# Layer 1 of a two-layer decoder: gates and half of the values by seven block products, all values through DRAM

## The chip, the core and the metric

The kernel runs on one core of a Trainium2 chip. The metric is the device time of one execution in microseconds. A difference of about 0.2% is what a measurement of this kernel can tell from no change.

The names used below are those of the profile: PE is TensorE (matmuls), PEld its weight loads, DVE is VectorE, ACT is ScalarE, POOL is GpSimd, and SP is SyncE, which here only issues DMAs.

## What is computed

Two layers over 512 rows of width 1024. Layer 1 is a differential attention of 16 heads, layer 2 a spatial gating MLP. The change is in layer 1:

```python
h = rms_norm(x, attn_norm)                       # 512 x 1024
proj = h @ w_in                                  # 1024 x 8192: q, k, v, gate, 2048 columns each
q, k, v, gate = ...                              # 16 heads; q and k hold two halves of 64, v is 128 wide
s  = softmax(q1 @ k1.T * scale + bias) - lam * softmax(q2 @ k2.T * scale + bias)   # causal
o  = rms_norm(s @ v, subln) * (1 - lam_init)
x  = x + (o * silu(gate)) @ w_out
```

All data are float32. Each product with a weight is made of three: both operands are cut into a high part (`hi`) and the rest (`lo`), and hi·hi + lo·hi + hi·lo is summed in PSUM.

## The kernel before

**Weights.** A weight comes from DRAM in chunks of 1 MB, in two halves (tile `raw`, three halves held). ACT rounds each of four pieces to `hi` (L134) and DVE makes `lo = raw - hi` (L135). There are three `hi`/`lo` pairs. `Chunk.tick` spreads the four pieces of the next chunk over the matmuls of the present one.

**Stages of layer 1.** `norm_rows` makes `hT` (hi and lo of the normed rows, turned). Then: `project_values(0)`, the values of heads 0 to 3 (96 matmuls of 512 columns, L423); `project_qk(0)`, q and k of heads 0 and 1 (96 matmuls, L253 to L255, tile `psqk`); the gate loop, 16 blocks of 24 matmuls into `psg`, each ended by a SiLU into `yT` (L501 to L506); then eight pairs of heads.

**A pair of heads.** `attention_steps` (L606) lays five groups of score blocks over ten slots: in slot t `scores` of group t (tile `pss`, L562), in slot t+2 `flip` (transposes of the finished weights, tile `pa`, L589), in slot t+3 `values` (tile `po`, L600); after `values` of the last group of a head `normalise` runs, and `close` (transposes of `on`, tile `pto`, L540) stands in slot 6 for the first head and in slot 9 for the second. I number the events: scores 0 to 4, flip 0 to 4, values 0 to 4, close 1 and close 2. Between PE's `scores` and `flip` of a group lies the softmax: DVE adds the bias and takes the maximum (L572), ACT takes the exponential (L575), DVE takes the reciprocal, scales and subtracts (L579 to L583). Between `values` and `close` lie four squares on ACT (L530), eleven small DVE operations that make a reciprocal root (L185 to L197), and one product into `on` (L534).

**Filler.** `interleave` (L620) puts projections for later heads between the slots, in units of three matmuls. Pairs 1 to 6 get 48 units each: 32 of `project_qk` for the next pair and 16 of `project_values` (`units`, L643), pairs 7 and 8 get 40, from `last_units`. The q and k results are written by ACT (`qkh`, L446) and DVE (`qkl`, L447). A scheduler then fixes one order of instructions for each engine before the run; each engine works its list off in that order. In the list, close 1 of pairs 1 to 7 follows values 3 at once.

**Block products.** Layer 2 already makes its input projection with `Quads` and seven products for each 1024 columns in the place of eight (the Strassen-Winograd form): a 512 by 512 quarter of the weight is loaded, sums and differences of quarters are made by DVE and by accumulating POOL DMAs (`quarter<-quarter`, 1 MB each), each form is cut into `hi` and `lo` (L344, L345), and the rows' sums `s1` to `s4` are made once. `product_n` has 24 matmuls of 512 columns, `product_t` 48 of 256 columns (L881).

Of the kernel before, what the change touches and what calls it, by code (L numbers as in the profile page):

```python
# [50 lines left out]
def build(ctx, tc, x, rel_bias, attn_norm, w_in, lq1, lk1, lq2, lk2, subln, w_out,  # L51
# [36 lines left out]
    v_at, qk_at = {0: add_values(0)}, {0: add_pair(0)}  # L88
    gate_at = len(chunks)
    for c in range(NH // 2):  # L90
        chunks.append(in_src(w_in, 3 * BR + c * 2 * P))
    for p in range(1, NH // 2):
        qk_at[p] = add_pair(p)
        if p % 2 and p < NH // 2 - 1:
            v_at[p // 2 + 1] = add_values(p // 2 + 1)
# [10 lines left out]
    limit = [sgu_at]  # L106
# [123 lines left out]
    def norm_rows(r, b):  # L230

        rs = row_scale(r, b, r > 0)
        xs = yT[:, 4 + 2 * (b % 2):6 + 2 * (b % 2), :].rearrange("p k n -> p (k n)")
        for m in range(2):
            ms = slice(m * S, (m + 1) * S)
            xs_last[0] = nc.vector.scalar_tensor_tensor(xs[:, ms], xr[:, b, ms], rs, gb[:, ms], ALU.mult, ALU.mult)
        sl = slice(b * P, (b + 1) * P)
        for q in range(KD // 4):
            pt = bank("ptx")
            for j in range(4):  # L240
                k = 4 * q + j
                nc.tensor.transpose(pt[:, j * P:(j + 1) * P], xs[:, k * P:(k + 1) * P], ident)
            pq = pt.rearrange("p (j n) -> p j n", n=P)
            hi_last[0] = nc.scalar.copy(hT[0][:, 4 * q:4 * q + 4, sl], pq)  # L244
            hT_last[0] = nc.vector.tensor_tensor(hT[1][:, 4 * q:4 * q + 4, sl], pq, hT[0][:, 4 * q:4 * q + 4, sl].bitcast(F32),
                                    ALU.subtract)

# [10 lines left out]

    def proj_n(ps, w, b, lo_last=False):

        bs = slice(b * P, (b + 1) * P)
        terms = ((0, w.hi), (0, w.lo), (1, w.hi))
        if lo_last:
            order = [(k, t) for t in (0, 2) for k in range(KD)] + [(k, 1) for k in range(KD)]
        else:
            order = [(k, t) for k in range(KD) for t in range(3)]
        n = len(order)
        for i, (k, t) in enumerate(order):
            a, m = terms[t]
            nc.tensor.matmul(ps, lhsT=hT[a][:, k, bs], rhs=m[:, k, :], start=(i == 0), stop=(i == n - 1))  # L270
            if i % 6 == 5:
                w.tick()
                yield
# [29 lines left out]


# [97 lines left out]
    def project_values(g, blocks, norm=None):  # L402

        i0 = v_at[g]
        if norm is not None:
            prepare(norm, 0)
            with tc.issue_after(xs_last[0].ins):
                for piece in range(PIECES):
                    split(i0, piece)
        if blocks[0] == 0:  # L410
            V[g] = att.tile([P, NB, S], F32, name="v"), [Chunk(i0, 8), None]
        v, w = V[g]
        for two in (blocks[i:i + 2] for i in range(0, len(blocks), 2)):
# [16 lines left out]
            for b in two:  # L430
                nc.scalar.copy(v[:, b, :], ps[b])
# [20 lines left out]
    run(project_qk(0))  # L452
# [7 lines left out]
    lt = yT[:, 12, 0:4 * HALF].rearrange("p (i h) -> p i h", i=4)  # L460
    for i, t in enumerate((lq1, lk1, lq2, lk2)):
        nc.scalar.dma_start(lt[:, i, :], t.broadcast_to([P, HALF]))
    lj = yT[:, 12, 4 * HALF:5 * HALF]
# [24 lines left out]
    oh = yT[0:NBUCK + 1, 0:2, :].rearrange("p k n -> p (k n)")[:, 0:TLEN]  # L488
    nc.scalar.dma_start(oh, onehot)
    tb = dram.tile([NH, TLEN], F32, name="tb")  # L490
    for c in range(2):
# [3 lines left out]
        tbs = yT[0:NH, 10 + c, 0:TLEN // 2]  # L495
# [5 lines left out]
    for c in range(NH // 2):  # L501
# [10 lines left out]
    class Head:  # L512
        def __init__(self, h):
            self.h = h
            qk, self.v = QK[h // 2], V[h // 4][0]
# [27 lines left out]
    class Group:  # L543
# [49 lines left out]
        def values(self):  # L593
            for hd, i, cs in self.parts:
# [68 lines left out]

    def sgu_quarter(n):
        def of(name):
            r, c = divmod("abcd".index(name), 2)
            return wide_src(sgu_w_in, r, columns[n] + c * S)[0]
        return of
# [10 lines left out]
    quads = Quads(qp, [sgu_quarter(n) for n in range(len(columns))])  # L679
# [5 lines left out]
    H = S // 2  # L685
    first = yT[:, 12:16, :].rearrange("p k n -> p (k n)").rearrange("p (k n) -> p k n", n=H)

    gb = yT[:, 6:8, :].rearrange("p k n -> p (k n)")
    last_mm = []
# [25 lines left out]

    def of_h(q, half):
        return [h[:, 4 * q:4 * q + 4, half * H:(half + 1) * H] for h in hT]

    def part(hi, lo, raw):
        nc.scalar.copy(hi, raw)  # L720
        nc.vector.tensor_tensor(lo, raw, hi.bitcast(F32), ALU.subtract)
# [52 lines left out]
    def product_n(ps, a, w, start):  # L774

        more = {} if start else {"skip_group_check": True}
        for i in range(2):
            rs = slice(i * P, (i + 1) * P)
            for k in range(4):
                nc.tensor.matmul(ps[i], lhsT=a[0][:, k, rs], rhs=w[0][:, k, :], start=(start and k == 0), stop=False, **more)  # L780
                nc.tensor.matmul(ps[i], lhsT=a[0][:, k, rs], rhs=w[1][:, k, :], start=False, stop=False, **more)
                last_mm[:] = [nc.tensor.matmul(ps[i], lhsT=a[1][:, k, rs], rhs=w[0][:, k, :], start=False,
                                               stop=(k == 3), **more)]
                yield

# [89 lines left out]
    def product_t(ps, a, w, start):  # L875

        for f in range(4):
            for k in range(4):
                for t, (x, y) in enumerate(((0, 0), (0, 1), (1, 0))):
                    clear = start and f % 2 == 0 and k == 0 and t == 0  # L880
                    nc.tensor.matmul(ps[f // 2][:, f % 2 * H:(f % 2 + 1) * H], lhsT=w[x][:, k, f * P:(f + 1) * P],  # L881
                                     rhs=a[y][:, k, :], start=clear, stop=(k == 3 and t == 2),
                                     skip_group_check=not (start and f % 2 == 0))
                yield

# [129 lines left out]
```

## Time and profile before

| what | value |
|---|---|
| median of 3 runs | 925.95 us (925.34 to 926.55) |
| the profiled execution | 928.58 us, its span 926.8 us |
| PE busy | 904.7 us, 98% of the span |
| DVE busy | 598.2 us, 65% |
| ACT busy | 446.1 us, 48% |
| granted PE clock, mean | 0.997 |

The profiled execution took 2.6 us more than the median of the runs; 1.8 us of it lie outside its span. PE's busy time is made of pipelined records whose ends are modelled, so a busy PE can hold short waits. Start-to-start distances tell more: within the gate loop a matmul starts every 0.227 us. All times of events below are microseconds from the start of the span.

### The profile page before, as it was taken

The page shows a single profiled execution, that of the slowest core. Times are in us where ns is not written, and L with a number is a line of the kernel's source. Part 1 is how long each engine was busy: PE and PEld are TensorE (multiplying, and loading weights), DVE is VectorE, ACT ScalarE, POOL GpSimd, SP SyncE. Part 2 cuts the span into 40 slices and gives each one's busy share as a digit, 9 for nine tenths or more (in the row PEclk, how much of TensorE's full clock was granted, in tenths as well). Part 3 has the DMA queues.
Part 4 walks back from the last instruction along what each step waited for, and adds up shares of the span by engine and source line. Part 5 has one row for each costly group of instructions (what it writes and reads, how often), then busy time and mean ns, then how long its engine had stood idle before and what let it go on. Part 6 is the DMA issues. An engine that isn't in the chain of part 4 may idle for free.

```text
span 926.8 us, 13474 instructions
## 1 busy us (share of the span) xinstructions
PE 904.7 (98%) x5129; PEld 768.6 (83%) x5129; DVE 598.2 (65%) x1359; ACT 446.1 (48%) x995; POOL 24.9 (3%) x38
## 2 busy tenths in 40 slices
PE   7999999999999999999999999999999999999996
PEld 4878887878787878787778887687999999998885
DVE  6532225666766676667777838885887777776634
ACT  6432225545454545454655616664554435454432
POOL 0000000000000000000000002000000000000000
PEclk9999999999999999999999999999999999999998
DMA  7433223213221332132212704647465564534202
GB/s 249 131 104 119 91 91 92 69 49 112 91 69 50 111 92 69 52 108 92 69 46 92 272 1 114 171 105 222 94 200 99 181 138 136 115 114 147 88 17 91
DMA packets 57904, 100.75 MB, mean 109 GB/s; under 512 B 3741, under 2 KB 28366, under 8 KB 56304
## 3 DMA queue, kind: packets, MB, share of 16 engines
q1 hardware_dynamic: 53216, 79.70, 26.5%
q0 software_dynamic: 3568, 18.88, 9.2%
q10 hardware_dynamic: 1056, 1.32, 0.5%
q8 instruction: 40, 0.66, 0.3%
q14 instruction: 24, 0.20, 0.1%
HBM read 85.17 MB, written 2.14 MB: 94 GB/s over the span
## 4 chain that ended last, share of the span: by engine, by line
PE 81%; DVE 10%; DMA 4%; ACT 3%; issue 1%; SPq 0%; ACTq 0%; POOLq 0%; DVEq 0%
PE psv L423 10%; PE px L881 10%; PE py L881 7%; PE psqk L253 6%; PE psqk L255 6%; PE psqk L254 6%; PE acc L289 5%; PE acc L288 5%; PE acc L290 5%; PE pss L562 3%; PE psg L253 3%; PE psg L254 3%; PE psg L255 3%; PE po L600 3%; DMA quarter<-quarter 3%; DVE lo L345 2%
## 5 line engine op out<-in xcount | busy, mean ns | idle before, releaser
L135 DVE TENSOR_TENSOR lo<-raw,hi 128x512 fp32r<-128x512 f32 x192 | 124.4, 687 | 104.4 <-ACT hi L134 104.2
L134 ACT CAST hi<-raw 128x512 fp32r<-128x512 f32 x192 | 109.4, 619 | 104.2 <-PE psqk L254 44.2
L345 DVE TENSOR_TENSOR lo<-quarter,hi 128x1024 fp32r<-128x1024 f32 x84 | 102.2, 1242 | 44.4 <-ACT hi L344 39.8
L344 ACT CAST hi<-quarter 128x1024 fp32r<-128x1024 f32 x84 | 85.9, 1047 | 93.0 <-DMA quarter<-quarter 36.6
L253 PE MATMUL psqk<-hT,hi 128*128 128x512 f32 x256 | 104.3, 408 | 0.0
L575 ACT ACTIVATE e<-e,nm 128x384 f32<-128x384 f32 (+3 forms) x128 | 70.6, 553 | 67.6 <-DVE nm L572 67.6
L255 PE MATMUL psqk<-hT,lo 128*128 128x512 f32 x256 | 100.2, 392 | 0.0
L254 PE MATMUL psqk<-hT,hi 128*128 128x512 f32 x256 | 99.9, 390 | 0.0
L423 PE MATMUL psv<-hi,hT 128*128 128x512 f32 x256 | 87.3, 408 | 1.9 <-ACT hT L244 1.9
L288 PE MATMUL acc<-hi,hT 128*128 128x512 f32 x224 | 88.1, 393 | 0.0
L290 PE MATMUL acc<-hi,hT 128*128 128x512 f32 x224 | 87.4, 390 | 0.0
L289 PE MATMUL acc<-lo,hT 128*128 128x512 f32 x224 | 87.3, 390 | 0.0
L881 PE MATMUL py<-hT,hi 128*128 128x256 f32 x384 | 69.9, 284 | 0.0
L572 DVE CUSTOM_DVE_ANT_0 e<-pss,bias 128x384 f32<-128x384 f32 (+3 forms) x128 | 55.7, 488 | 17.6 <-PE pss L562 17.4
L423 PEld LDWEIGHTS psv<-hi,hT 128*128 128x128 f32 x256 | 49.2, 192 | 15.4 <-ACT hT L244 2.5
L881 PEld LDWEIGHTS py<-hT,hi 128*128 128x128 f32 x384 | 59.8, 192 | 0.0
L253 PEld LDWEIGHTS psqk<-hT,hi 128*128 128x128 f32 x256 | 48.1, 188 | 13.0 <-issue 2.6
L255 PEld LDWEIGHTS psqk<-hT,lo 128*128 128x128 f32 x256 | 48.0, 188 | 10.5
L254 PEld LDWEIGHTS psqk<-hT,hi 128*128 128x128 f32 x256 | 48.2, 188 | 8.9
L881 PE MATMUL py<-hT,lo 128*128 128x256 f32 x192 | 54.3, 283 | 0.0
L283 DVE TENSOR_TENSOR hT<-yT,hT 128x512 fp32r<-128x512 f32 x56 | 37.5, 689 | 25.8 <-PE acc L289 17.3
L282 ACT CAST hT<-yT 128x512 fp32r<-128x512 f32 x56 | 33.1, 621 | 38.3 <-PE acc L289 28.2
(198 smaller groups left out, 1921.1 us busy)
## 6 DMA issues: line engine op xcount, KB each, us to landing
raw<-in_attn_w_in SPq DMA_DIRECT2D x62, 512.0 KB, 3.9
quarter<-in_sgu_w_in SPq DMA_DIRECT2D x48, 512.0 KB, 4.9
quarter<-quarter POOLq DMA_DIRECT2D x12, 1024.0 KB, 7.3
raw<-in_attn_w_out SPq DMA_DIRECT2D x16, 512.0 KB, 3.5
raw<-in_sgu_w_out SPq DMA_DIRECT2D x16, 512.0 KB, 3.6
bias<-tb POOLq DMA_DIRECT2D x16, 256.0 KB, 3.6
xr<-in_x SPq DMA_DIRECT2D x4, 512.0 KB, 5.0
out_y<-xr SPq DMA_DIRECT2D x8, 256.0 KB, 2.1
```

What stands on the lines that cost most here:

```text
L134: nc.scalar.copy(hi[:, sl], raw)
L135: nc.vector.tensor_tensor(lo[:, sl], raw, hi[:, sl].bitcast(F32), ALU.subtract)
L253: nc.tensor.matmul(ps, lhsT=w.hi[:, k, cs], rhs=hT[0][:, k, :], start=(k == 0), stop=False)
L254: nc.tensor.matmul(ps, lhsT=w.hi[:, k, cs], rhs=hT[1][:, k, :], start=False, stop=False)
L255: nc.tensor.matmul(ps, lhsT=w.lo[:, k, cs], rhs=hT[0][:, k, :], start=False, stop=(k == KD - 1))
L288: nc.tensor.matmul(acc[b], lhsT=yh[:, j, bs], rhs=w.hi[:, j, :], start=(k == 0), stop=False)
L289: nc.tensor.matmul(acc[b], lhsT=yh[:, j, bs], rhs=w.lo[:, j, :], start=False, stop=False)
L290: nc.tensor.matmul(acc[b], lhsT=yl[:, j, bs], rhs=w.hi[:, j, :], start=False, stop=(k == KB - 1))
L344: nc.scalar.copy(hi[:, sl], raw[:, sl])
L345: nc.vector.tensor_tensor(lo[:, sl], raw[:, sl], hi[:, sl].bitcast(F32), ALU.subtract)
L423: nc.tensor.matmul(ps[b], lhsT=hT[a][:, k, bs], rhs=m[:, j, :], start=(k == 0 and a == 0 and m is w[half].hi), stop=(k == KD - 1 and a == 1))
L881: nc.tensor.matmul(ps[f // 2][:, f % 2 * H:(f % 2 + 1) * H], lhsT=w[x][:, k, f * P:(f + 1) * P], rhs=a[y][:, k, :], start=clear, stop=(k = ...
```

## The change

Columns of the gates (2048) and of the values of heads 8 to 15 (1024) are now made in three passes of `Quads`, seven products each: pass 0 (values) with `product_n`, passes 1 and 2 (gates) with `product_t`. The row sums for it are made by the new `row_sums` beside the values of heads 4 to 7. All values are made ahead of the attention. They are put into `yT`, stored to DRAM (`vd`, four DMAs of 1 MB from POOL's queue) and fetched again for four heads at a time (`fetch_values`, 1 MB, POOL's queue). The order of stages is now: values 0 to 3, values 4 to 7, three passes of block products, `project_qk(0)`, eight pairs. The filler of pairs 1 to 6 is `project_qk` alone, 32 units.

```diff
-    v_at, qk_at = {0: add_values(0)}, {0: add_pair(0)}
...
+    v_at = {g: add_values(g) for g in range(2)}
+    qk_first = len(chunks)
+    qk_at = {p: add_pair(p) for p in range(NH // 2)}
...
+            if b < 2:
+                nc.scalar.copy(first[:, 4 * q:4 * q + 4, hs], pq)
...
+    def row_sums(b):
...
+        nc.scalar.copy(t, pq[1])
+        nc.vector.tensor_tensor(t, pq[0], t, ALU.add)
+        nc.vector.tensor_tensor(u, f[:, 0:4], t, ALU.subtract)
...
+    def save_values(g):
+        nc.gpsimd.dma_start(vd[g], yT[:, 4 * g:4 * g + 4, :].rearrange("p k n -> p (k n)"))
...
-                nc.scalar.copy(v[:, b, :], ps[b])
+                nc.scalar.copy(yT[:, 4 * g:4 * g + 4, b * P:(b + 1) * P], of_bank(ps[b]))
+        save_values(g)
...
-    run(project_qk(0))
...
+    quads = Quads(qp, [columns_of(w_in, n0) for n0 in (2 * BR + D, 3 * BR, 3 * BR + D)])
+    beside(project_values(1, range(NB)), (u for g in (row_sums(2), row_sums(3), quads.work(0), quads.work(1)) for u in g))
...
-    for c in range(NH // 2):
-        w = Chunk(gate_at + c, 16)
-        for j in range(2):
-            ps = bank("psg")
-            run(proj_t(ps, w, j))
-            nc.scalar.activation(yT[:, 2 * c + j, :], ps, AF.Silu)
+    for n in range(3):
+        gates, m = n > 0, n - 1
...
+        for i in range(7):
+            work = quads.work(7 * n + i + 2)
...
+            product = product_t if gates else product_n
+            beside(product(py if i in (1, 3, 6) else px, sides[i], quads.forms[n, i], i in (0, 1, 3)), work)
...
+        if not gates:
+            for g in (2, 3):
+                save_values(g)
...
+    def fetch_values(g):
+        V[g] = att.tile([P, 4, NB, P], F32, name="v")
+        nc.gpsimd.dma_start(V[g].rearrange("p j b n -> p (j b n)"), vd[g])
+
+    fetch_values(0)
+    run(project_qk(0))
...
+        if p % 2 and p < NH // 2 - 1:
+            fetch_values(p // 2 + 1)
         if p < NH // 2 - 1:
-            interleave(steps, units(p), 48)
+            interleave(steps, project_qk(p), 32)
```

The scheduler lays all lists anew. Three places show what the pairs get. On DVE, in pair 3, from the last step of group 4's softmax (`e`) to the chain that ends in `on` of the first head (`rv`, `ry`, `ru` are its small tiles, `lo` a piece of a weight chunk). Before:

```order
L583 SCALAR_TENSOR_TENSOR e_2291<-e_2292,r_2304,e_2291 128x128
L447 SCALAR_TENSOR_TENSOR qkl<-psqk,qkh 128x512
L197 TENSOR_SCALAR rv_2344<-ssq 128x4
L185 TENSOR_SCALAR ry_2346<-rv_2344 128x4
L190 TENSOR_TENSOR ru_2347<-ry_2346,rv_2344 128x4
L191 TENSOR_TENSOR ru_2347<-ru_2347,ry_2346 128x4
```

and after the change (its lines differ, its names do not):

```order
L715 SCALAR_TENSOR_TENSOR e_2868<-e_2869,r_2881,e_2868 128x128
L505 SCALAR_TENSOR_TENSOR qkl<-psqk,qkh 128x512
L130 TENSOR_TENSOR lo<-raw,hi 128x512
L192 TENSOR_SCALAR rv_2916<-ssq 128x4
L180 TENSOR_SCALAR ry_2918<-rv_2916 128x4
L130 TENSOR_TENSOR lo<-raw,hi 128x512
L185 TENSOR_TENSOR ru_2919<-ry_2918,rv_2916 128x4
L130 TENSOR_TENSOR lo<-raw,hi 128x512
L186 TENSOR_TENSOR ru_2919<-ru_2919,ry_2918 128x4
L130 TENSOR_TENSOR lo<-raw,hi 128x512
L187 SCALAR_TENSOR_TENSOR ry_2918<-ru_2919,ry_2918 128x4
```

Four `lo` pieces have moved from the place ahead of group 4's softmax (L135 at 262.80 in the trace) to behind it, three of them into the chain itself; pairs 2 to 6 read alike.

On PE, in the same pair, around close 1. Before:

```order
L255 MATMUL psqk<-hT_103,lo 128x512
L589 MATMUL pa<-ident,e_2291 128x128 x4
L600 MATMUL po<-v,at 128x128 x4
L540 MATMUL pto<-flip,on 128x128 x4
L253 MATMUL psqk<-hT_103,hi 128x512
```

and after:

```order
L254 MATMUL psqk<-hT_103,hi 128x512
L255 MATMUL psqk<-hT_104,hi 128x512
L256 MATMUL psqk<-hT_103,lo 128x512
L672 MATMUL pto<-flip,on 128x128 x4
L732 MATMUL po<-v,at 128x128 x4
L254 MATMUL psqk<-hT_103,hi 128x512
```

Close 1 now stands nine filler matmuls behind flip 4 and values 3, and just ahead of values 4. From scores 0 of the pair to the next pair's, the runs of filler matmuls have now 9, 9, 9, 9, 12, 9, 9, 20 and 10 (before: 12, 15, 15, 15, 15, 12, 15, 30 and 15). They stand ahead of scores 1, flip 0 with scores 2, flip 1 with scores 3, flip 2 with scores 4, flip 3, flip 4, close 1 (before: values 4), close 2 and the next scores 0.

On POOL, whose list is its DMA queue, from the constants to layer 2. Before:

```order
masks.py:199 ISA
masks.py:199 AFFINE_SELECT ident<-ident 128x128
L523 DMA bias<-tb 128x512 x16
L336 DMA quarter<-quarter 128x2048
L855 DMA wst<-in_sgu_w_s 128x16x128
```

and after, from the last store of values on:

```order
L451 DMA vd<-yT 128x2048
L365 DMA quarter<-quarter 128x2048 x3
L635 DMA v<-vd 128x2048 x2
L655 DMA bias<-tb 128x512 x6
L635 DMA v<-vd 128x2048
L655 DMA bias<-tb 128x512 x4
L635 DMA v<-vd 128x2048
L655 DMA bias<-tb 128x512 x6
```

The third and fourth fetch of values stand behind the biases of the heads that start next.

## Rows read from the trace of the kernel before

**Rows 1.** The page, part 1: busy time, share of the span, instructions of each engine.

```profile
PE 904.7 (98%) x5129; PEld 768.6 (83%) x5129; DVE 598.2 (65%) x1359; ACT 446.1 (48%) x995; POOL 24.9 (3%) x38
```

**Rows 2.** Stretches: from:to, length, busy by engine, granted clock, DMA share, GB/s.

```profile
62.80:150.10 87.30, 87.30 (x387) 72.01 (x386) 21.24 (x34) 26.09 (x48) 1.27 (x2) 1.00 0.33 103
150.10:427.50 277.40, 277.40 (x1561) 227.40 (x1560) 185.22 (x599) 142.36 (x428) 6.46 (x12) 1.00 0.26 80
427.50:521.00 93.50, 91.03 (x511) 74.09 (x511) 75.76 (x228) 58.89 (x167) 1.08 (x2) 1.00 0.31 102
656.50:831.00 174.50, 174.50 (x1474) 174.50 (x1473) 133.23 (x163) 81.26 (x107) 7.78 (x9) 1.00 0.53 140
```

**Rows 3.** Gate loop, tile psg: count, least/median/most ns, first to last start, form.

```profile
L253 PE MATMUL psg<-hT,hi x128: 389/389/499, 62.8 to 149.3; 128*128 128x512 f32 x128
```

**Rows 4.** Timeline of PE, layer 2, four products apart: start, us, instruction, count.

```profile
697.92 0.40 PE L881 MATMUL py<-hT,hi 128*128 128x256 f32 x2
...
720.88 0.40 PE L881 MATMUL py<-hT,hi 128*128 128x256 f32 x2
```

**Rows 5.** Layer 2: a wait of PE (timeline, idle before in brackets); accumulating DMAs (page).

```profile
648.16 0.50 PE L780 MATMUL px<-hi,s4h 128*128 128x512 f32 x1 [1.72 <-ACT yT L798]
...
quarter<-quarter POOLq DMA_DIRECT2D x12, 1024.0 KB, 7.3
```

**Rows 6.** Timeline of PE, pair 3: scores 0, flip 1, close 1, values 4, close 2, next scores 0.

```profile
242.70 0.50 PE L562 MATMUL pss<-qkh 64*128 64x512 f32 x2
...
256.10 0.60 PE L589 MATMUL pa<-ident,e 128*128 128x128 f32 x4
...
273.33 0.60 PE L540 MATMUL pto<-flip,on 128*128 128x128 f32 x4
...
277.22 1.05 PE L600 MATMUL po<-v,at 128*128 128x128 f32 x8
...
284.93 0.60 PE L540 MATMUL pto<-flip,on 128*128 128x128 f32 x4
...
288.91 0.50 PE L562 MATMUL pss<-qkh 64*128 64x512 f32 x2
```

**Rows 7.** Timeline of DVE, pair 3: softmax of group 1, then the second head's chain.

```profile
252.43 0.88 DVE L583 SCALAR_TENSOR_TENSOR e<-e,r,e 128x384 f32<-128x384 f32 x2
...
280.33 0.16 DVE L191 TENSOR_TENSOR ru<-ru,ry 128x4 f32<-128x4 f32 x1
280.41 0.69 DVE L135 TENSOR_TENSOR lo<-raw,hi 128x512 fp32r<-128x512 f32 x1
281.01 0.16 DVE L192 SCALAR_TENSOR_TENSOR ry<-ru,ry 128x4 f32<-128x4 f32 x1
...
282.39 0.69 DVE L534 TENSOR_TENSOR on<-po,rso 128x512 f32<-128x512 f32 x1
```

**Rows 8.** Timeline of PE, pair 7: scores 0 and close 1.

```profile
427.53 0.50 PE L562 MATMUL pss<-qkh 64*128 64x512 f32 x2
...
457.05 0.63 PE L540 MATMUL pto<-flip,on 128*128 128x128 f32 x4 [1.45 <-DVE on L534]
```

**Rows 9.** Timeline of DVE, pair 7: groups 1, 3, 4, then the first head's chain.

```profile
437.24 0.88 DVE L583 SCALAR_TENSOR_TENSOR e<-e,r,e 128x384 f32<-128x384 f32 x2
...
442.87 0.68 DVE L572 CUSTOM_DVE_ANT_0 e<-pss,bias 128x512 f32<-128x512 f32 x1
...
446.67 0.68 DVE L135 TENSOR_TENSOR lo<-raw,hi 128x512 fp32r<-128x512 f32 x1
...
449.67 0.55 DVE L572 CUSTOM_DVE_ANT_0 e<-pss,bias 128x384 f32<-128x384 f32 x1
...
453.25 0.88 DVE L583 SCALAR_TENSOR_TENSOR e<-e,r,e 128x384 f32<-128x384 f32 x2
...
454.04 0.17 DVE L197 TENSOR_SCALAR rv<-ssq 128x4 f32<-128x4 f32 x1
...
456.22 0.69 DVE L534 TENSOR_TENSOR on<-po,rso 128x512 f32<-128x512 f32 x1
```

More of the change, by code (lines that the diff above doesn't have):

```diff
@@ L257, in proj_t @@
             yield
[L259 to L273, printed above, removed]
     def out_half(i0, m, store, cs=range(4), acc=None, finish=None):
@@ L302, in hT_store, with of_h, part, product_n @@
         return hT[0][:, o:o + 4, :], hT[1][:, o:o + 4, :]
+    H = S // 2
+    last_mm = []
+    first = yT[:, 12:16, :].rearrange("p k n -> p (k n)").rearrange("p (k n) -> p k n", n=H)
+    def of_h(q, half):
+        return [h[:, 4 * q:4 * q + 4, half * H:(half + 1) * H] for h in hT]
+    def part(hi, lo, raw):
+        nc.scalar.copy(hi, raw)
+        nc.vector.tensor_tensor(lo, raw, hi.bitcast(F32), ALU.subtract)
+    def product_n(ps, a, w, start):
+        more = {} if start else {"skip_group_check": True}
+        for i in range(2):
+            rs = slice(i * P, (i + 1) * P)
+            for k in range(4):
+                nc.tensor.matmul(ps[i], lhsT=a[0][:, k, rs], rhs=w[0][:, k, :], start=(start and k == 0), stop=False, **more)
+                nc.tensor.matmul(ps[i], lhsT=a[0][:, k, rs], rhs=w[1][:, k, :], start=False, stop=False, **more)
+                last_mm[:] = [nc.tensor.matmul(ps[i], lhsT=a[1][:, k, rs], rhs=w[0][:, k, :], start=False,
+                                               stop=(k == 3), **more)]
+                yield
+    def product_t(ps, a, w, start):
+        for f in range(4):
+            for k in range(4):
+                for t, (x, y) in enumerate(((0, 0), (0, 1), (1, 0))):
+                    clear = start and f % 2 == 0 and k == 0 and t == 0
+                    nc.tensor.matmul(ps[f // 2][:, f % 2 * H:(f % 2 + 1) * H], lhsT=w[x][:, k, f * P:(f + 1) * P],
+                                     rhs=a[y][:, k, :], start=clear, stop=(k == 3 and t == 2),
+                                     skip_group_check=not (start and f % 2 == 0))
+                yield
+    def of_bank(ps):
+        return ps.rearrange("p (g c) -> p g c", c=P)
+    def temp():
+        return wraw.tile([P, 2, S], F32, tag="raw", name="raw")
+    def hold(t, ps):
+        for f in range(2):
+            nc.scalar.copy(t[:, f], ps[f])
     class Quads:
@@ L499, in build, with place, to_yT, aside @@
     late.close()
-    for c in range(NH // 2):
-        w = Chunk(gate_at + c, 16)
-        for j in range(2):
-            ps = bank("psg")
-            run(proj_t(ps, w, j))
-            nc.scalar.activation(yT[:, 2 * c + j, :], ps, AF.Silu)
+    sides = [of_h(0, 0), of_h(1, 0), sums["s2"], sums["s3"], sums["s1"], sums["s4"], of_h(1, 1)]
+    px, py = [[bank(t) for _ in range(2)] for t in ("px", "py")]
+    for n in range(3):
+        gates, m = n > 0, n - 1
+        if gates:
+            t1, t4, t2 = (temp() for _ in range(3))
+        def place(c, half, i):
+            g = 8 + 4 * c
+            return yT[:, g:g + 4, (2 * half + i) * P:(2 * half + i + 1) * P]
+        def to_yT(c, half, ps, t=None, add=True):
+            for f in range(2):
+                if not gates:
+                    y = place(c, half, f)
+                    if add:
+                        nc.vector.tensor_tensor(y, of_bank(ps[f]), y, ALU.add)
+                    else:
+                        nc.scalar.copy(y, of_bank(ps[f]))
+                    continue
+                v = ps[f]
+                if add:
+                    nc.vector.tensor_tensor(t[:, f], ps[f], t[:, f], ALU.add)
+                    v = t[:, f]
+                g = 8 * m + 4 * c + 2 * f
+                nc.scalar.activation(yT[:, g:g + 2, half * H:(half + 1) * H], v.rearrange("p (j n) -> p j n", n=H),
+                                     AF.Silu)
+        def aside(t, c, half, ps):
+            if gates:
+                hold(t, ps)
+            else:
+                to_yT(c, half, ps, None, False)
+        for i in range(7):
+            work = quads.work(7 * n + i + 2)
+            if n == 2 and i == 5:
+                limit[0] = sgu_at
+                load(qk_first)
+            if n == 2 and i > 4:
+                work = (split(qk_first, 2 * (i - 5) + h) for h in range(2))
+            product = product_t if gates else product_n
+            beside(product(py if i in (1, 3, 6) else px, sides[i], quads.forms[n, i], i in (0, 1, 3)), work)
+            if i == 0:
+                aside(t1 if gates else None, 0, 0, px)
+            if i == 1:
+                to_yT(0, 0, py, t1 if gates else None)
+            if i == 2:
+                aside(t2 if gates else None, 0, 1, px)
+            if i == 4:
+                aside(t4 if gates else None, 1, 1, px)
+                to_yT(1, 1, py, t4 if gates else None)
+            if i == 5:
+                to_yT(1, 0, px, None, False)
+            if i == 6:
+                to_yT(0, 1, py, t2 if gates else None)
+        if not gates:
+            for g in (2, 3):
+                save_values(g)
@@ L678, in build @@
     acc = [bank(f"acc{b}") for b in range(NB)]
-    quads = Quads(qp, [sgu_quarter(n) for n in range(len(columns))])
+    quads = Quads(qp, [columns_of(sgu_w_in, n0) for n0 in columns])
     gen = out_half(i0 + 4, 1, lambda c: (hT_store if c < 2 else yp_store)(c), range(4), acc,
                    residual(1, 1, acc))
-    H = S // 2
-    first = yT[:, 12:16, :].rearrange("p k n -> p (k n)").rearrange("p (k n) -> p k n", n=H)
     gb = yT[:, 6:8, :].rearrange("p k n -> p (k n)")
-    last_mm = []
+    last_mm.clear()
     turned = [[bank("ptx") for _ in range(2)]]
@@ L714, in rows @@
         return b, pq
[L716 to L721, printed above, removed]
     for c in range(4):
@@ L772, in build @@
     sides = [of_h(0, 0), of_h(1, 0), sums["s2"], sums["s3"], sums["s1"], sums["s4"], of_h(1, 1)]
[L774 to L784, printed above, removed]
     vss = const.tile([P, NB, BR // S], F32, name="vss")
@@ L872, in build @@
         nc.vector.tensor_scalar(yT[:, :, sl], yT[:, :, sl], vrs[:, b:b + 1], None, ALU.mult)
[L875 to L884, printed above, removed]
     px, py = [[bank(t) for _ in range(2)] for t in ("px", "py")]
```

85 lines of the change are left out of this document (45 added, 40 removed).

## The prediction

> **What bounds the kernel now.** I read the page's busy times first: PE is busy for 98% of the span, DVE for 65% [rows 1]. Then the stretches: in the gate loop (62.8 to 150.1) and in pairs 1 to 6 (150.1 to 427.5) PE is busy all the time, and DVE for 24% and 67% of it [rows 2]. So there a microsecond of PE work saved is a microsecond won, as long as nobody makes PE wait. Pairs 7 and 8 with what follows them (427.5 to 521.0) have less filler, and there PE is idle for 2.5 us of 93.5 [rows 2]. Hence the second view, the timelines of PE and DVE in a pair with 48 filler units (pair 3) and in one with 40 (pair 7). In pair 3 no event of PE waits [rows 6]; in pair 7 close 1 waits 1.45 us for DVE's `on` [rows 8]. The reader is to see in the two that DVE's chain through a pair takes its own time, counted from scores 0, and that filler is what covers it. Times with a plus below are counted from the start of scores 0 of the pair.
>
> **PE's work.** Removed are 384 matmuls of the gates and 192 of the values of heads 8 to 15, all of 512 columns. In the gate loop 127 triples lie between starts at 62.8 and 149.3, so 0.227 us for one [rows 3]: 576 x 0.227 = 130.8. Added are 7 products of 24 such matmuls, 7 x 24 x 0.227 = 38.1, and 14 products of 48 matmuls with 256 columns. Of these, four take from 697.92 to 720.88, 5.74 each (0.1196 for one matmul) [rows 4]: 80.4. Net: 118.5 - 130.8 = -12.3 us. The seven products of `product_t` take 40.2 against 43.6 for the eight blocks they replace, 8% and not an eighth, because half the columns cost more than half the time.
>
> A rule bears on this price. The Trainium skill (TensorE: Matmul & The Clock Gate, Back-to-back issue gap) gives 262 cycles for 256 columns, at 2.4 GHz an estimated 109 ns. The trace disagrees with 119.6 ns [rows 4], and the row is of the same form. By the page the change would be 672 x 0.0104 = 7 us better than by the row; this stands among the rivals.
>
> **The stages ahead of the pairs.** `project_qk(0)` trades places with the values of heads 4 to 7, 96 matmuls each, at no cost. The extra work of ACT and DVE there (four copies of `first`, the row sums, the first splits) goes beside 192 PE matmuls, 43.6 us, in a kernel that uses DVE at 65%. In the passes, DVE has the same splits and subtractions as in layer 2, where it is busy for 133.2 of 174.5 us while PE has no idle time [rows 2]. The four stores of values, 1 MB each, share POOL's queue with the accumulating DMAs, whose median is 7.3 us [rows 5]; a store ahead of one delays the splits that wait for it on ACT and DVE, and through them PE. The forms are made two products ahead (11 us), which covers one such delay. If the cover is gone, the nearest row is PE's wait of 1.72 us in layer 2 at such a place [rows 5]. I take +1 for all seams, with 0 and 4 as ends (nothing, or a wait like that at two places and some loss at the start). The fetches of values go out behind the biases that the next heads need, and nobody on POOL is queued behind them that is needed soon; the first has the 21.8 us of `project_qk(0)` ahead of its use, against 7.3 us for 1 MB on this queue. Cost 0; with no cover it would be 7, once.
>
> **The pairs.** This is where the gain has to survive. Pairs 1 to 6 lose 48 filler matmuls each, 10.9 of the 46.2 us [rows 6]; that saving is already in the sum above, or was moved ahead. What is left, 35.3 us, is PE's time only if DVE keeps up. I follow pair 2 to 6 in the new lists.
>
> Flip 1: in pair 3 PE reaches it at +13.40 [rows 6] with 42 filler matmuls behind it; now 27, so at 13.40 - 15 x 0.227 = +10.0. Group 1 is ready when its last `e` ends, at 252.43 + 0.88 = 253.31, +10.6 [rows 7]; in pair 7, where flip 1 is earlier, again at 437.24 + 0.88 - 427.53 = +10.6 [rows 8, 9]. DVE's list up to there is the same as now. So PE waits, 0.75 us for the last of four transposes with a semaphore's 0.15 (457.05 less the end of `on`, 456.91 [rows 8, 9]); the first three start as soon as the first of two parts is there, 0.3 earlier: 0.5.
>
> Close 1: PE reaches it at 273.33 - 242.70 = +30.63 with 84 filler matmuls behind it, now 66: 30.63 - 4.08 + 0.5 = +27.05. DVE: group 3 begins at 442.87, +15.34 in pair 7, with the same list ahead of it but for one `qkl` that has moved inside; it ends at 446.67, where pair 7 has three microseconds of `lo` and `qkl` until group 4 begins at 449.67 [rows 9]. The new list has group 4 there at once, at +19.14. From its begin to its last `e` is 454.13 - 449.67 = 4.46, so +23.6. In pair 7 the chain begins then, and from `rv` at 454.04 to the end of `on` at 456.91 it takes 2.87 [rows 9]. The new list puts `qkl` and one `lo` ahead of it (0.6 each) and three `lo` into it; one such costs 0.48, from 280.41 to 281.01 in the place of the 0.12 until 280.53 [rows 7]. So `on` ends at 23.5 + 1.2 + 2.87 + 1.44 = +29.05, and PE starts close 1 at +29.2. Wait: 2.15 us. Queued behind it on PE are values 4, the filler and close 2; nothing on PE can pass it.
>
> Close 2: values 4 to close 2 is 284.93 - 277.22 = 7.71 in pair 3, with 30 filler matmuls; with 20 it is 5.44. The chain from values 4 to the end of the second `on` takes 283.08 - 277.22 = 5.86 with one `lo` in it [rows 6, 7]; the new list has one `qkl` there, the same. Wait: 5.86 + 0.15 - 5.44 = 0.55.
>
> Together 0.5 + 2.15 + 0.55 = 3.2 us in a pair, six times 19.2. The ends: 2.0 a pair if `lo` finds time ahead of the chain (12 in all), 4.2 if ACT's copies and squares, which I count as hidden, add 1.0 (25). No waits of pairs 1 to 6 go away for it, since there are next to none, and pairs 7 and 8 keep their list.
>
> **The sum.** -12.3 + 1 + 19.2 = +7.9 us, so 936.5 for the profiled execution of 928.58. That one lies 2.6 above the median of the runs; on the median, 925.95 + 7.9 = 933.9.
>
> **Rivals.** (1) *The pairs keep up.* DVE and ACT are idle for a third and half of a pair [rows 2], so slack is there; if the `lo` pieces cost the chain nothing and close 1 finds `on` ready, what is left is flip 1 and close 2 at 0.5 each, 6 us in all, and the time is 925.95 - 12.3 + 1 + 6 = 920.7. It decides at 1.9 us of waits a pair: below that the change wins. Against it: the lists are fixed, DVE works them off in order, and the same steps have the same length in pairs 3 and 7. (2) *The passes wait too.* The splits of a pass hang on accumulating DMAs behind stores; at a wait of 1.72 [rows 5] three times in a pass, six or so in all count, 10 us are added to the forecast: 944. For it: it happened in layer 2 with no stores in the queue. Against: once, and not in the 174.5 us of 256-column products [rows 2]. (3) *Products with 256 columns at the page's gap:* 933.9 - 7 = 926.9, no change. Against it stands the trace.
>
> **How the numbers follow.** Forecast 0.76, rival 1 0.13, rival 2 0.08, rival 3 0.03. A difference of 0.2%, 1.85 us, is about what a measurement can tell. The forecast's own ends are 925.95 - 12.3 + 0 + 12 = 925.7 and 925.95 - 12.3 + 4 + 25 = 942.7, so a twentieth of it lies within 0.2%: slower 0.80, same 0.07, faster 0.13. The range holds 8 in 10 with 922 to 942; rival 1's lower half and most of rival 2 are left out.
>
> **What would show it.** Right: pairs 1 to 6 at about 38.5 us from scores 0 to scores 0, close 1 with an idle time of about 2 us released by DVE's `on`, PE busy nearly without a gap from 62 to 203, and scores 0 of pair 1 at about 204. Wrong: pairs of 36.5 us or less (rival 1); PE waiting for `hi` or `lo` of a quarter (rival 2); products of `product_t` at 5.2 us (rival 3). The forecast fails as a whole if DVE's first half of a pair, up to group 4's end at +23.6, comes out more than 1.5 us earlier, since everything behind it is counted from there.

## The result: 1.2% slower

| what | before | after |
|---|---|---|
| median of 4 runs | 925.64 us (924.60 to 926.55) | 936.75 us (936.22 to 936.94) |
| ratio | | 1.0119 (1.0102 to 1.0137) |
| the profiled execution | 928.58 us, span 926.8 | 936.22 us, span 934.5 |

The change costs 11.1 us; I had forecast 933.9 us, 7.9 more than before, with slower at 0.80. The spans of the profiled executions differ by 7.7 us. Most of the document is about the pairs, where the work that PE was spared came back as waiting; the 3.4 us between 7.7 and 11.1 have a part of their own at the end of the experiments.

The page of the changed kernel, part 1 (answers [rows 1]):

```profile
PE 898.9 (96%) x5393; PEld 772.1 (83%) x5393; DVE 649.0 (69%) x1399; ACT 474.5 (51%) x1015; POOL 34.3 (4%) x52
```

PE is busy 5.8 us less than before, and is idle for 35.6 us where it was idle for 22. The stretches say where, in the columns of [rows 2]: the three passes, `project_qk(0)`, pairs 1 to 6, and pairs 7 and 8 with what follows:

```profile
62.00:181.00 119.00, 119.00 (x841) 111.26 (x839) 70.23 (x71) 60.91 (x80) 8.10 (x12) 1.00 0.61 173
181.00:203.20 22.20, 22.20 (x101) 18.17 (x101) 8.78 (x14) 7.80 (x16) 0.00 (x0) 1.00 0.77 249
203.20:435.50 232.30, 218.38 (x1273) 173.99 (x1272) 167.65 (x576) 121.86 (x392) 7.52 (x14) 0.99 0.25 78
435.50:528.70 93.20, 90.78 (x510) 73.91 (x510) 75.47 (x227) 58.86 (x167) 1.08 (x2) 1.00 0.29 101
```

In the passes PE does not wait. In pairs 1 to 6, where before it was busy for 277.40 of 277.40 us, it is now idle for 13.9 of 232.3. PE's timeline of pair 3 (scores 0, flip 1, close 1, values 4, close 2, next scores 0; answers [rows 6]):

```profile
280.92 0.50 PE L694 MATMUL pss<-qkh 64*128 64x512 f32 x2
...
291.30 0.66 PE L721 MATMUL pa<-ident,e 128*128 128x128 f32 x4 [0.23 <-DVE e L715]
...
310.06 0.63 PE L672 MATMUL pto<-flip,on 128*128 128x128 f32 x4 [1.95 <-DVE on L666]
310.52 1.06 PE L732 MATMUL po<-v,at 128*128 128x128 f32 x8
316.33 0.63 PE L672 MATMUL pto<-flip,on 128*128 128x128 f32 x4 [0.18 <-DVE on L666]
319.20 0.50 PE L694 MATMUL pss<-qkh 64*128 64x512 f32 x2
```

A pair takes 38.28 us. Close 1 starts at +29.14 and has waited for `on`; before, it stood at +30.63, had 18 more filler matmuls of its pair ahead of it, and waited for nothing [rows 6]. What DVE did meanwhile, from the end of group 4's softmax to `on` (answers [rows 9]):

```profile
303.63 0.87 DVE L715 SCALAR_TENSOR_TENSOR e<-e,r,e 128x384 f32<-128x384 f32 x2
304.43 0.68 DVE L505 SCALAR_TENSOR_TENSOR qkl<-psqk,qkh 128x512 fp32r<-128x512 f32 x1
305.03 0.68 DVE L130 TENSOR_TENSOR lo<-raw,hi 128x512 fp32r<-128x512 f32 x1
305.63 0.16 DVE L192 TENSOR_SCALAR rv<-ssq 128x4 f32<-128x4 f32 x1
...
305.90 0.68 DVE L130 TENSOR_TENSOR lo<-raw,hi 128x512 fp32r<-128x512 f32 x1
...
309.22 0.69 DVE L666 TENSOR_TENSOR on<-po,rso 128x512 f32<-128x512 f32 x1
```

The reader sees a chain of small steps with one `qkl` and four `lo` pieces of the next weight chunk in or ahead of it. `lo` waits for nobody here and is needed by nobody for ten microseconds; it stands in the list ahead of steps that PE waits for.

### The profile page after: what moved, and what is told of

It reads as the page before. It is cut to its first block, busy times and chain, and to the rows that moved or that the text cites. A ratio compares the mean times of both kernels' runs of the same rounds, so it can differ in the third digit from the quotient of the medians.

```text
span 934.5 us, 14107 instructions
## 1 busy us (share of the span) xinstructions
PE 898.9 (96%) x5393; PEld 772.1 (83%) x5393; DVE 649.0 (69%) x1399; ACT 474.5 (51%) x1015; POOL 34.3 (4%) x52
## 4 chain that ended last, share of the span: by engine, by line
PE 62%; DVE 23%; ACT 8%; DMA 4%; issue 3%; SPq 0%; ACTq 0%; POOLq 0%; DVEq 0%
PE px L319 15%; PE py L319 11%; PE acc L273 5%; PE acc L274 5%; PE acc L275 5%; ACT e L707 5%; DVE lo L130 4%; PE psv L480 3%; DMA quarter<-quarter 3%; DVE e L715 3%; PE psqk L254 2%; PE psqk L255 2%; PE psqk L256 2%; DVE e L704 2%; DVE e L714 2%
## 5 line engine op out<-in xcount | busy, mean ns | idle before, releaser
L374 DVE TENSOR_TENSOR lo<-quarter,hi 128x1024 fp32r<-128x1024 f32 x126 | 152.7, 1234 | 87.3 <-ACT hi L373 86.9
L373 ACT CAST hi<-quarter 128x1024 fp32r<-128x1024 f32 x126 | 128.8, 1047 | 125.9 <-DMA quarter<-quarter 40.8
L130 DVE TENSOR_TENSOR lo<-raw,hi 128x512 fp32r<-128x512 f32 x144 | 94.2, 684 | 37.4 <-ACT hi L129 37.2
L129 ACT CAST hi<-raw 128x512 fp32r<-128x512 f32 x144 | 81.5, 621 | 67.2 <-PE psqk L255 37.1
L254 PE MATMUL psqk<-hT,hi 128*128 128x512 f32 x256 | 107.1, 418 | 0.0
L255 PE MATMUL psqk<-hT,hi 128*128 128x512 f32 x256 | 101.1, 395 | 0.0
L319 PE MATMUL py<-hT,hi 128*128 128x256 f32 x512 | 93.0, 283 | 0.0
L319 PEld LDWEIGHTS py<-hT,hi 128*128 128x128 f32 x512 | 79.7, 192 | 0.0
L319 PE MATMUL py<-hT,lo 128*128 128x256 f32 x256 | 72.4, 283 | 0.0
L256 PEld LDWEIGHTS psqk<-hT,lo 128*128 128x128 f32 x256 | 48.7, 190 | 10.8
L273 PEld LDWEIGHTS acc<-hi,hT 128*128 128x128 f32 x224 | 42.1, 188 | 9.4 <-issue 0.7
L275 PEld LDWEIGHTS acc<-hi,hT 128*128 128x128 f32 x224 | 42.1, 188 | 9.0
```

Source lines behind the costliest of these rows:

```text
L129: nc.scalar.copy(hi[:, sl], raw)
L130: nc.vector.tensor_tensor(lo[:, sl], raw, hi[:, sl].bitcast(F32), ALU.subtract)
L254: nc.tensor.matmul(ps, lhsT=w.hi[:, k, cs], rhs=hT[0][:, k, :], start=(k == 0), stop=False)
L255: nc.tensor.matmul(ps, lhsT=w.hi[:, k, cs], rhs=hT[1][:, k, :], start=False, stop=False)
L256: nc.tensor.matmul(ps, lhsT=w.lo[:, k, cs], rhs=hT[0][:, k, :], start=False, stop=(k == KD - 1))
L273: nc.tensor.matmul(acc[b], lhsT=yh[:, j, bs], rhs=w.hi[:, j, :], start=(k == 0), stop=False)
```

## The experiments

The theory: DVE works its list off in order, so the chain to `on` gets longer by every piece that the list puts in or ahead of it, and with 32 filler units a pair no longer covers it. The main rivals: too little filler in whatever order, and a loss in the passes. Times with a plus count from scores 0 of the pair.

**e3: values ahead, no block products.** Layer 1 with the old gate loop; all values by ordinary products ahead of it.

```diff
-    quads = Quads(qp, [columns_of(w_in, n0) for n0 in (2 * BR + D, 3 * BR, 3 * BR + D)])
...
+    for g in range(1, NH // 4):
+        run(project_values(g, range(NB)))
...
+    for c in range(NH // 2):
+        w = Chunk(gate_at + c, 16)
+        for j in range(2):
+            ps = bank("psg")
+            run(proj_t(ps, w, j))
+            nc.scalar.activation(yT[:, 2 * c + j, :], ps, AF.Silu)
```

> No block products in layer 1: the gate loop of before, and all values made ahead by ordinary products, stored and fetched as in the changed kernel; pairs 1 to 6 have 32 units. As many matmuls as in the kernel before. Theory: all six pairs lose about 3.4 us, nothing is saved: 925.64 + 20 = 946, and the changed kernel against it is the worth of the block products, -11 or so. Rival A (the loss belongs to the passes): pairs lose less, below 938.

Measured: 946.89 us, 1.0238 of before (1.0208 to 1.0268). Pairs 1 to 6 take 232.3 us as in the changed kernel. Two of its pairs (4 and 5), columns of [rows 2]:

```profile
330.97:369.28 38.31, 35.91 (x213) 28.58 (x213) 27.92 (x96) 20.04 (x66) 1.61 (x3) 1.00 0.31 97
369.28:408.80 39.52, 37.33 (x213) 29.88 (x213) 28.00 (x96) 20.03 (x66) 1.07 (x2) 0.96 0.22 67
```

Against the kernel before of the same set of runs (925.78) the loss is 21.1 us, and 20.3 of it lie in the pairs: it comes with the filler that was taken from them. Scores 0 of pair 7 stands at 447.09 here and at 435.53 in the changed kernel: the block products are worth 11.6 us, where I had 12.3 less 1 for the seams.

**e2: gates alone by block products.** Two passes; values of heads 8 to 15 are filler of pairs 3 to 6 again.

```diff
-    quads = Quads(qp, [columns_of(w_in, n0) for n0 in (2 * BR + D, 3 * BR, 3 * BR + D)])
+    quads = Quads(qp, [columns_of(w_in, n0) for n0 in (3 * BR, 3 * BR + D)])
...
-            interleave(steps, project_qk(p), 32)
+            interleave(steps, units(p), 48 if p > 2 else 32)
```

> Only the gates by block products (two passes); values of heads 0 to 7 ahead, those of heads 8 to 15 by ordinary products in pairs 3 to 6 again, which have 48 units; pairs 1 and 2 have 32. Theory (a pair with 32 units loses about 3.4 us, one with 48 nothing; the passes gain what the rows say): 925.64 - 6.8 + 1 + 2 x 3.4 = 926.6, pairs 3 to 6 at 46.2, pairs 1 and 2 at 38.3 to 39.5. Rival A (the loss lies in the passes and their seams): above 930, with PE idle between the values and the first pair. Rival B (the loss in the pairs is not one of the 32 units): pairs 3 to 6 wait as well, 933 or more.

Measured: 928.0 us, 1.0018 (1.0004 to 1.0032). Pair 1 (32 units) and pair 3 (48 units):

```profile
165.23:203.48 38.25, 35.89 (x214) 28.62 (x213) 28.01 (x96) 21.64 (x67) 1.08 (x2) 1.00 0.23 70
...
243.08:289.29 46.21, 46.21 (x262) 37.90 (x262) 31.38 (x101) 23.33 (x71) 1.08 (x2) 1.00 0.27 80
```

In one and the same execution the pairs with 48 units wait for nothing, and the two with 32 take 38.25 and 39.60. Scores 0 of pair 7 comes 0.8 us later than in a second profile of the kernel before (427.91 and 427.12), where 1.0 was expected. The time was expected at 926.6 and is 928.0, 2.2 more than the kernel before of the same set (925.78): the rest lies behind the pairs, 1.0 of it in one wait of layer 2 (1.65 us here, 0.63 in that second profile). Both rivals of this expectation fall.

**e1: the pieces moved into the softmax.** All work of the changed kernel, PE's list in pairs 1 to 6 unchanged. The eight pieces of a pair go behind the row maxima of groups 0 to 4 and ahead of their reciprocals; close 1 is held at its place. The edit:

```diff
+            for g, (c, pieces) in {0: (1, (0, 1)), 1: (1, (2, 3)), 2: (2, (0,)), 3: (2, (1, 2)), 4: (2, (3,))}.items():
+                groups[g].pieces = [(qk_at[p] + c, k) for k in pieces]
...
+            for _, rest in puts:
+                with tc.issue_after(top.ins):
+                    first_put.enter_context(tc.issue_after(rest().ins))
...
-        slots[6].append((3, one.close))
+        slots[7].append((0.5, one.close))
```

> The changed kernel with the pieces (hi and lo) of a pair's own second weight chunk and of the next pair's first put into the softmax of groups 0 to 4 (2, 2, 1, 2, 1 pieces), behind the row maxima and ahead of the reciprocal, where DVE waits about a microsecond for ACT; close 1 is held at its place in PE's list. PE's list in the pairs is the same as in the changed kernel, nothing of DVE's work is gone. Theory (the lo pieces inside the chain to `on` set close 1): the chain starts behind one qkl, `on` ends at about +26.9, close 1 starts at about +27.1 and not +29.1; with 0.3 for flip 1, 0.3 for close 1 and 0.5 for close 2 a pair takes 36.4 and not 38.7, and the time is 936.75 - 14 = 923. Rival A (32 units are too little filler in whatever order): pairs stay at 38 or more, 933 to 937. Rival B (a piece in a softmax costs it its full 0.6 us): the chain starts as late as it did, flips wait, pairs of 37.5, 929.

Measured: 923.55 us, 0.9978 (0.9963 to 0.9993), 13 us less than the changed kernel with the same instructions. DVE's timeline of pair 3 (scores 0 at 276.55), from group 4 to `on`:

```profile
296.65 0.69 DVE L130 TENSOR_TENSOR lo<-raw,hi 128x512 fp32r<-128x512 f32 x1
297.98 0.18 DVE L726 RECIPROCAL r<-l 128x4 f32<-128x4 f32 x1 [0.64 <-ACT e L718]
...
298.85 0.88 DVE L730 SCALAR_TENSOR_TENSOR e<-e,r,e 128x384 f32<-128x384 f32 x2
299.64 0.68 DVE L511 SCALAR_TENSOR_TENSOR qkl<-psqk,qkh 128x512 fp32r<-128x512 f32 x1
300.48 0.17 DVE L195 TENSOR_SCALAR rv<-ssq 128x4 f32<-128x4 f32 x1 [0.16 <-ACT on L668]
...
302.67 0.69 DVE L672 TENSOR_TENSOR on<-po,rso 128x512 f32<-128x512 f32 x1
```

and PE's close 1:

```profile
303.51 0.63 PE L679 MATMUL pto<-flip,on 128*128 128x128 f32 x4 [0.24 <-DVE on L672]
```

The reciprocal still waits 0.64 us for ACT's exponential behind the piece, so this piece cost nothing. Close 1 stands at +26.96 and not at +29.14. That is as the theory has it; rival A (the amount of filler) and rival B (a piece costs its full time) fall. The total came out as expected only in part for the expected reason: pairs 1 to 6 took 221.5 us, 10.8 less and not 14, and 2.6 were won in pairs 7 and 8, where the held close no longer waits (before 1.45 us in pair 7 [rows 8] and 0.73 in pair 8). The missing part lies in pair 1 (37.7 us) and in pair 6. Pair 3, which is as it should be, and pair 6:

```profile
276.55:312.65 36.10, 35.67 (x213) 28.68 (x212) 28.32 (x96) 20.12 (x66) 1.08 (x2) 1.00 0.26 74
...
385.06:424.25 39.19, 37.20 (x213) 29.93 (x212) 30.44 (x100) 20.13 (x66) 1.08 (x2) 0.96 0.32 94
```

Pair 6 has 100 instructions on DVE and not 96: four pieces of pair 7's second chunk had moved up into its chain, its close 1 waits 1.99 us, and it is as long as the longest pairs of the changed kernel, with the same mean clock of 0.96 (the last section).

**e5: the other two pairs.** As e1, with those four pieces in groups 0 and 1 of pair 7, and each group's softmax ended before the next begins (in pair 1 a row maximum had stood ahead of the end of group 1).

```diff
+        if p == NH // 2 - 1:
+            placed.add(qk_at[p])
+            for g in range(2):
+                groups[g].pieces = [(qk_at[p] + 1, 2 * g + k) for k in range(2)]
...
+                    with tc.issue_after(last_s[0].ins) if last_s else ExitStack():
```

> As e1_lo_in_gaps, with its two odd pairs put right: in pair 6 four lo pieces of pair 7's second chunk still stood in the chain to `on` (pair 6 took 39.19 us, with a wait of 1.99 at close 1), here they go into groups 0 and 1 of pair 7; in pair 1 a row maximum of group 2 stood ahead of the end of group 1's softmax (37.74, flip 1 waited 1.70), here each group ends before the next begins. Theory: both take 36.1 to 36.3, and the time is 923.55 - 2.9 - 1.6 = 919, faster than both kernels. Rival (pair 6 is long because of pair 7's other filler, pair 1 because of its start): 922 to 924.

Measured: 918.8 us, 0.9920 (0.9905 to 0.9934): faster than both kernels. Its pairs 1 and 6 and the page's part 1:

```profile
201.98:237.89 35.91, 35.71 (x214) 28.70 (x214) 28.29 (x96) 21.43 (x67) 1.07 (x2) 1.00 0.26 74
...
382.46:418.53 36.07, 35.66 (x214) 28.69 (x214) 28.29 (x96) 20.12 (x66) 1.07 (x2) 1.00 0.26 74
```

```profile
PE 894.6 (98%) x5393; PEld 769.2 (84%) x5393; DVE 651.0 (71%) x1399; ACT 474.5 (52%) x1015; POOL 34.6 (4%) x52
```

All six pairs now take 35.9 to 36.3, against 35.3 of PE's own work.

**e4: close 1 earlier in PE's list.** As e1, without the hold: close 1 stands two filler matmuls behind values 3, and not nine. The edit is shown against e1:

```diff
-        slots[7].append((0.5, one.close))
+        slots[6].append((3, one.close))
```

> As e1_lo_in_gaps, DVE's list in pairs 1 to 6 word for word the same, but close 1 is not held: in PE's list it stands two filler matmuls behind values 3 and not nine, with seven between it and values 4. Theory (PE works its list off in order, so an event that is early in the list waits, and what is behind it waits too): `on` ends at +26.8 as before, PE reaches close 1 7 x 0.227 = 1.6 us earlier and waits that much longer, values 4 and with it the second chain start 1.6 later, a pair takes 37.7 and not 36.1, and the time is 923.55 + 6 x 1.6 = 933; in pair 7 the wait of 1.45 at close 1 is back. Rival (only DVE's order counts, PE catches up with its filler): 924.

Measured: 934.77 us, 1.0099 (1.0066 to 1.0133). Close 1 of pair 3:

```profile
305.55 0.63 PE L675 MATMUL pto<-flip,on 128*128 128x128 f32 x4 [1.82 <-DVE on L669]
```

Pairs 2 to 5 took 37.7 to 37.9, as expected. Close 1 starts at the same +26.9 in both; PE comes to it 1.6 us earlier and cannot use the filler that stands behind. So moving the pieces is worth 13 us with close 1 held and 2 us without: the length of DVE's chain and the place of the event in PE's list count together.

**e6: the pieces behind `on`.** The changed kernel with close 1 held and the four pieces out of the first chain, but into the second.

```diff
-                if self.t >= self.n * (p + 1) // (PIECES + 1):
-                    split(self.i + 1, p)
+                if self.t >= (4 + 2 * p if late else self.n * (p + 1) // (PIECES + 1)):
+                    with tc.issue_after(last_on[0].ins) if late else ExitStack():
+                        split(self.i + 1, p)
```

> The changed kernel with close 1 held at its place, and the lo pieces of the next pair's first chunk moved out of the first head's chain, but to the place behind `on` and into the second head's chain (four behind `on`, two with a qkl in the second chain, two behind its end), none into a softmax; close 2 has 24 filler matmuls ahead of it. Theory (a piece costs what it displaces, and only a place where DVE waits for ACT is free): close 1 at +27 without a wait, but two pieces in the second chain cost 0.5 each, close 2 waits 1.2 to 1.5 where it waited 0.35, a pair takes 37, and the time is 923.55 + 0.9 x 5 = 928. Rival (any place outside the first head's chain does it): 923 to 924.

Measured: 931.72 us, 1.0059 (1.0044 to 1.0074), pairs of 37.8 to 38.1 (pair 1: 39.9) and not 37. Close 1 came at +26.7 to +26.9 in pairs 3 to 6, as expected, but close 2 started 1.8 to 2.4 us (pair 1: 2.7) later than the matmul ahead allows, and not 1.2 to 1.5. DVE and ACT in the second chain of pair 3:

```profile
313.07 0.16 DVE L189 SCALAR_TENSOR_TENSOR ry<-ru,ry 128x4 f32<-128x4 f32 x1
315.09 0.69 DVE L131 TENSOR_TENSOR lo<-raw,hi 128x512 fp32r<-128x512 f32 x1 [1.86 <-ACT hi L130]
```

```profile
314.44 0.62 ACT L130 CAST hi<-raw 128x512 fp32r<-128x512 f32 x1 [2.25 <-DMA raw<-in_attn_w_in]
```

The rival's 923 to 924 falls for this list, but my reason was wrong too: I counted 0.5 for a piece, and this one was not ready. A `raw` half is loaded when an earlier one is split, and that had been put off too; `lo` then waited 1.86 us (1.3 to 2.2 in the six pairs) with the rest of the chain behind it. A step that is moved takes the wait for its own input with it. What a piece that is ready costs in the second chain, e6 does not show.

**e0, e8, e7: the other 3 us.** The kernel before (e0) and the changed one (e8) were profiled a second time, unchanged, and e7 puts 14 more DMAs of 1 MB on POOL's queue of the kernel before.

> The kernel of before once more, for a second profile of it: the first profiled execution took 928.58 us, 2.6 above the median of the other runs, and which stretch they lie in could not be seen from one trace. If they are one execution's own, this one takes 925 to 926 us and the stretches show where the first lost 2.6; if the profile itself costs them, it takes 928 to 929 again, and the changed kernel's profiled 936.22 (0.5 below its own median) speaks against it.

> The changed kernel once more, for a second profile of it. If the wait of layer 2's second product belongs to the kernel, it is there again, behind an accumulating DMA of about 9.2 us, and the span is 934 to 935; if it falls out by chance, one in two has none, and the span is about 932.7. Scores 0 of pair 1 at 203.2 and of pair 7 at 435.5, to 0.5 us, either way, with the granted clock at half after one or two of the waits at close 1.

```diff
+        for i in range(2 * c - 2, 2 * c):
+            if c:
+                nc.gpsimd.dma_start(scrap[i], yT[:, 2 * c - 2:2 * c + 2, :].rearrange("p k n -> p (k n)"))
```

> The kernel before with 14 more DMAs on POOL's queue during the gate loop (1 MB each, from yT to a scratch place in DRAM, two behind each SiLU block), so that this queue has carried as many DMAs ahead of layer 2 as in the changed kernel; nothing reads what they store. It tells where the changed kernel's part of the difference comes from that lies in layer 2, where the second product waits about 2 us in five of five profiles of kernels with three passes, and in one of two of the kernel before. Theory A (what the queue has carried before sets how long its accumulating DMAs take): the first of them in the second product takes 9.2 us and not 7, the wait is there, and the time is 927.5 to 928. Theory B (it is not the queue's history): accumulating DMAs of 7.0 and 8.5 us, no wait in most executions, 925.7 to 926.

Measured: e0 took 926.09 us with a span of 924.4, e8 938.59 with 936.9, e7 926.93, 1.0003 of before (0.9992 to 1.0015). In the pairs the profiles of one kernel agree to 0.1 us (scores 0 of pair 7 at 435.53 and 435.52). From the last matmul of the last close to the end they do not: 417.3 and 415.3 us before, 417.0 and 419.4 after. Most of it hangs on one wait in the second pass of layer 2's block products. In the changed kernel, ACT's wait for an accumulating DMA and, behind it, PE's:

```profile
641.67 1.05 ACT L373 CAST hi<-quarter 128x1024 fp32r<-128x1024 f32 x1 [8.70 <-DMA quarter<-quarter]
...
655.80 0.50 PE L307 MATMUL px<-hi,s4h 128*128 128x512 f32 x1 [1.54 <-ACT yT L893]
```

It is the wait of [rows 5]; e0 does not have it. Ahead of it stand two accumulating DMAs, which took 7.3 and 10.6 us in the first profile of before, 6.9 and 8.5 in e0, and 9.2 and 8.2 in the changed kernel. ACT's `hi` waits for them 9.13 us in the first profile of before, 8.70 and 8.73 in the two of the changed kernel, and 6.66 in e0. e8 missed its expected span of 934 to 935: its wait of PE is 0.8 us longer (2.31), and the clock fell behind it. So my base, the first profile, had 2 us in it that e0 has not; e0's 926.09 us lie near the kernel's medians (925.64 to 926.6), so its typical run, as far as the times tell, has not either. The changed kernel had a wait like it in both of its profiles. e7's profile has the wait as well (1.54 us), with DMAs of 7.2 and 10.5 us as in the first profile of before, and not the 9.2 that its theory A expected; the time did not change. So the history of POOL's queue is not the reason. Why the first of the two takes 9.1 to 9.2 us in both profiles of the changed kernel and in those of e1, e4 and e6 (e5 has 7.6 and 11.4, and the wait), stays open.

## Why the prediction was right

**Work.** Forecast -12.3. The passes run from 62.50 to 181.32, 118.8 us for 118.5. Passes 1 and 2 alone, from the first start to that of the next stage (PE's timeline, answers [rows 4]):

```profile
101.35 0.40 PE L319 MATMUL px<-hT,hi 128*128 128x256 f32 x2
...
181.32 0.40 PE L254 MATMUL psqk<-hT,hi 128*128 128x512 f32 x1
```

79.97 us for 80.4. That is 0.119 us a matmul; rival 3, which had 0.109, falls. The Trainium skill's 262 cycles (TensorE: Matmul & The Clock Gate, Back-to-back issue gap) are its gap of an isolated matmul; for a stream of weight loads and matmuls, which these are, the same section says that both set the spacing, and it has no figure for 256 columns. The prediction took the first for a rule on the second; the measurement decides.

**Seams.** Forecast +1, ends 0 and 4. Scores 0 of pair 1: 150.09 of before, plus 288 matmuls moved ahead (65.4), less 12.3, is 203.2; it stands at 203.20, so 0. Rival 2, waits in the passes, did not occur.

**Pairs.** Forecast +19.2, measured 232.3 - (277.4 - 65.4) = +20.3. The steps: flip 1 at +10.4, 0.39 us later than the matmul ahead allows (0.5), with `e` ready at +10.6 as forecast; group 4's end at +23.58 (forecast +23.6); `on` at +28.99 (+29.05, though the terms written there add up to +29.01); close 1 at +29.14 (+29.2), 2.11 us later than the matmul ahead allows (2.15); close 2 0.34 late (0.55). Undisturbed pairs take 38.3, 3.0 above 35.3, which makes 17.9 in six. What I did not have is in pairs 2 and 5, which take 39.5: the clock, below, 2.4 us in all. So the mechanism is as forecast and step by step near in size; that +20.3 is so near to +19.2 is partly luck.

**Sum.** +8.0 from the steps, +7.9 forecast, with 1 us too much for the seams and 1 too little for the pairs; the spans of the two profiles differ by 7.7. The step that failed is the last one, "on the median, 925.95 + 7.9": it takes for granted that what made the profiled run of before 2.6 us longer than the median is in neither kernel's typical run. Against e0 it is 0.4 us at the start and 2 us in the layer 2 wait of [rows 5], and the changed kernel keeps that wait. So the time came out 2.9 us above the forecast. I had the row in hand and used it as a bound for another stage, without asking whether it is in the median.

**Rival 1**, that the pairs keep up, was wrong for this list and right for another: with the pieces out of the chain and close 1 held (e5) the pairs take 36.1, and the time is 918.8, against the 920.7 of that rival. About 2 us of the 918.8 come from pairs 7 and 8, which that rival left as they were.

## What to carry to other kernels

Work that hides a chain has to be counted against the chain's own length before it is moved: each 32-unit pair of e2 waits and none of its 48-unit pairs does, and what a busy engine saves beyond that point comes back as waiting. When filler shrinks, read the other engines' lists for work that nobody waits for and that stands in a chain somebody waits for; put it where that engine waits anyway (e1, e5), with its own inputs in time (e6). And look whether a stall in the base profile is in every execution before a sum is laid on the median.

## What had not been expected of the hardware

A short wait can cost twice. In pair 2 of the changed kernel close 1 waits 1.95 us, and from 1.2 us behind the end of that wait TensorE's granted clock is at half, 1.2 GHz and not 2.4, for 3.41 us. The pair, the next one, a stretch of the former behind its wait, and PE's timeline there:

```profile
241.43:280.92 39.49, 37.32 (x213) 29.85 (x212) 27.98 (x96) 20.02 (x66) 1.61 (x3) 0.96 0.29 94
280.92:319.20 38.28, 35.92 (x215) 28.59 (x214) 27.89 (x96) 20.04 (x66) 1.07 (x2) 1.00 0.23 70
```

```profile
272.00:274.00 2.00, 2.00 (x7) 1.61 (x6) 0.38 (x3) 1.14 (x8) 0.53 (x1) 0.50 0.26 56
```

```profile
270.56 0.63 PE L672 MATMUL pto<-flip,on 128*128 128x128 f32 x4 [1.95 <-DVE on L666]
...
272.95 0.63 PE L256 MATMUL psqk<-hT,lo 128*128 128x512 f32 x1
273.37 0.63 PE L254 MATMUL psqk<-hT,hi 128*128 128x512 f32 x1
...
276.27 0.40 PE L254 MATMUL psqk<-hT,hi 128*128 128x512 f32 x1
276.51 0.39 PE L255 MATMUL psqk<-hT,hi 128*128 128x512 f32 x1
```

At half a matmul starts every 0.43 us, at full every 0.23; the pair is 1.2 us longer. The clock fell after nine of the 18 waits of about 2 us at close 1 (start to start 2.33 to 2.46) in the profiles of the changed kernel, e1, e2, e3 and e4, in both profiles of the changed kernel in pairs 2 and 5, and after none of the shorter waits there. It fell twice more: in e6 after the longest wait at a close 2 (2.91, in pair 1; not after the other five of 2.04 to 2.65), and in e8 after the layer 2 wait (2.71). Apart from the kernel's start and end these are all its falls in the eleven profiles, each 0.6 to 1.3 us behind the end of such a wait. That half the rate is the state without activity, and that activity releases it, is what the Trainium skill says (TensorE: Matmul & The Clock Gate, Part 1: The HAM clock gate); the two levels of the rows agree. Which of the waits brings it down cannot be told from their length, since pairs 3, 4 and 6 wait as long and keep the full clock.
